# A long convolution's table products as three rounded products in place of one fp32 product

## The chip, the cores and the metric

One core of one Trainium2 chip runs the whole program. The metric is the device time of one execution in microseconds (us). The engines are TensorE (PE; its weight loads are listed apart as PEld), VectorE (DVE), ScalarE (ACT), GpSimd (POOL) and SyncE (SP), which issues most loads.

## The reference

Two layers of a mixed backbone over 640 tokens: 512 latent tokens and 128 context tokens, width 1024. A layer is a feed-forward, a mixer and a second feed-forward. In the mixer one projection feeds three groups of channels: pooling, attention and "Hyena". The last is what matters here; it runs two long convolutions one behind the other, each over the whole sequence:

```python
def fft_conv(z, k):
    L = z.shape[1]
    zf = jnp.fft.rfft(z, n=2 * L, axis=1)
    kf = jnp.fft.rfft(k, n=2 * L, axis=0)
    return jnp.fft.irfft(zf * kf[None], n=2 * L, axis=1)[:, :L]

def hyena_mixer(u, sw, sb, filt, bias_d):
    uc = short_conv(u, sw, sb).astype(F32)
    v, x1, x2 = jnp.split(uc, 3, axis=-1)
    bd = bias_d.astype(F32)
    z = v
    for o, gate in enumerate((x1, x2)):
        z = gate * (fft_conv(z, filt[:, o]) + bd[o] * z)
    return z.astype(u.dtype)
```

## The kernel before

All weight products are three products of rounded parts: a weight tile of 128x512 is loaded (raw), ACT casts it to fp32r (whi, L294), DVE subtracts (wlo, L295), and PE adds hi x hi, lo x hi and hi x lo in fp32r. Each record `mm<-hhi,whi` with 320 columns is one of these. The tokens are the columns, 640 in two halves.

A long convolution has no FFT: the transforms are products with tables of cosines and sines. The generator `conv_step_old` does one convolution of 256 channels (two tiles) for the latent tokens and, with a small table kept in a constant, for the context:

- It asks for four forward tables (tab, 256 KB each, `load_full`, SP's queue) and five tiles of the filter's spectrum (kf), transposes even and odd tokens (ztp) and copies them (zt).
- zf: for two halves of the frequencies (fi = 0, 1) and two parities (pa), four fp32 products of 256 columns. One fp32 product stands in the trace as two records. ACT copies the odd part (zod), DVE adds and subtracts (zp, zm), multiplies by the spectrum (`cmul`: cw, cy) and combines (pp, pmn).
- It asks for four inverse tables, multiplies the context's part (zfc, zcs, cw, cy), and transforms back: yt, 16 fp32 products, and ytc, the context's. ACT scales (yv), DVE adds the bias term and multiplies by the gate (yu, yw).

A layer's two convolutions run one behind the other, as one of several generators (hyena, pooling, attention) whose steps are laid between the weight products by an order written out by hand (the string PROP), fixed when the program is built. Instructions run on each engine in that order. k and q are normalised (nps, qbc, u at L1297) and rotated (L1304 to L1307, "rope") on DVE in the same stretches, and the pooling of two channel groups (pl, pc, pw, pd, L1166 to L1185) stands there too: its small memsets are POOL's, a copy is ACT's, the sums are DVE's.

All these tiles (tables, spectra, zt, pp, pw, ...) come from one pool of 45 buffers (SLOTS, tag "s"). Whoever takes a buffer waits for the last reader of what was in it. The mixer chooses the convolution and, in the attention's step, transposes v (vt) right behind the second one.

Of the kernel before, what the change touches and what calls it, by code (L numbers as in the profile page):

```python
# [11 lines left out]
F32 = mybir.dt.float32  # L12
# [35 lines left out]
PVSKEW = 1  # L48
AHD = 2
PROP = "TGTTTTGGTGSGGGGTGTSTGTGTGSTGTGGSXTSGTSQGQDTGTQGGTTDDSTGTTQGSQGTDDTDTQQSGQQGQQDDQQDDDGTRQGSSDTSGDGGNDQNQSTTTGDGQDTSGQTDTGSGDDQGQDGTQSTQGDNGD"  # L50
CONV3 = 0
SQN = 3
TABX = 1
ADAW = (1.0, 1.25, 2.0, 0.75)
# [128 lines left out]
def hybrid_kernel(ctx: ExitStack, tc: tile.TileContext, a, depth=2, fc=22):  # L183
    nc = tc.nc
    V, S, G, DMA = nc.vector, nc.scalar, nc.gpsimd, nc.sync
# [78 lines left out]
    def load_tables(name, h, n, new=slot):  # L264

        ts = []
        for q in range(n):
            t = new(512, F32R, name="tab")
            DMA.dma_start(out=t.bitcast(F32), in_=a[name][h, q])
            ts.append(t.rearrange("p (h c f) -> p h c f", h=2, c=2))  # L270
        return ts

# [701 lines left out]
    def conv_step(l, o, z, gate, out):  # L974
        rl, rlc = filt[l]
        tf = [load_tables("fwd", 0, 4)]
        kf = filter_tiles(l, o)
        hb = PR(l, "hb")
# [15 lines left out]
        for fi in range(2):  # L994
            eo = []
            for pa in range(2):
                ps = mix(512, "zf")
                for c in range(2):
                    for i in range(2):
                        triple(ps[:, c * 256:(c + 1) * 256], [tf[fi][pa * 2 + i][:, h, c] for h in range(2)],  # L1000
                               [t[:, i, :] for t in zt[pa]], i == 0, i == 1)
                eo.append(ps)
            od = slot(512, name="zod")
            S.copy(out=od, in_=eo[1])
            zp, zm = slot(512, name="zp"), slot(512, name="zm")
            V.tensor_tensor(out=zp, in0=od, in1=eo[0], op=ALU.add)
            V.scalar_tensor_tensor(out=zm, in0=od, scalar=-1.0, in1=eo[0], op0=ALU.mult, op1=ALU.add)
            y = cmul(zp, kf[fi], o, 0)
            yp = cmul(zm, kf[2 + fi], o, 1)
            pp, pm_ = slot3(2, 256, name="pp"), slot3(2, 256, name="pmn")  # L1010
            for q in range(2):
                V.tensor_tensor(out=pp[:, q], in0=y[:, q], in1=yp[:, 1 - q], op=ALU.add)
                V.tensor_tensor(out=pm_[:, q], in0=y[:, q], in1=yp[:, 1 - q], op=ALU.subtract)
            hl = []
            for p_ in (pp, pm_):
                hl.append((slot3(2, 256, F32R, "ph"), slot3(2, 256, F32R, "pl")))
                split(p_, *hl[-1])
            pq.append(hl)
            if fi == 0:
                tf.append(load_tables("fwd", 1, 4))  # L1020
            if fi == 0:
                yield
        ti, vs = [load_tables("back", 0, 4)], []
        psc = mix(512, "zfc")
        for c in range(2):
# [119 lines left out]
    def short_conv(l, ci, u):  # L1145
        sw, sb = PR(l, "sw"), PR(l, "sb")
        t = slot(T, name="sc")
        S.activation(out=t, in_=u, func=AF.Identity, bias=sb[:, ci:ci + 1], scale=sw[:, 6 + ci:7 + ci])
        for c0, c1 in SEG:
            V.scalar_tensor_tensor(out=t[:, c0 + 1:c1], in0=u[:, c0:c1 - 1], scalar=sw[:, ci:ci + 1],  # L1150
                                   in1=t[:, c0 + 1:c1], op0=ALU.mult, op1=ALU.add)
            V.scalar_tensor_tensor(out=t[:, c0:c1 - 1], in0=u[:, c0 + 1:c1], scalar=sw[:, 12 + ci:13 + ci],
                                   in1=t[:, c0:c1 - 1], op0=ALU.mult, op1=ALU.add)
        return t
# [3 lines left out]
    def mixer(l, cur, nxt):  # L1158
# [90 lines left out]
        def need(name):  # L1249
            while name not in made:  # L1250
                next(stream)
            return made[name]
# [227 lines left out]
        def hyena():  # L1480
            zs = [short_conv(l, i, need(f"v{i}")) for i in range(2)]
            for o, (ci, ns) in enumerate(((2, ("xa", "xb")), (4, ("xc", "xd")))):
                out = []
                gate = lambda: [short_conv(l, ci + i, need(n)) for i, n in enumerate(ns)]
                yield from (conv_step if CONV3 else conv_step_old)(l, o, zs, gate, out)
                zs = out
# [320 lines left out]
```

## Time and profile before

| | us |
|---|---|
| median of 3 runs | 2418.3 (2416.39 to 2420.72) |
| the profiled execution | 2417.21 |
| its span, first to last instruction | 2415.4 |
| PE busy in it | 2369.8 (98%) |
| DVE busy | 1920.3 (80%) |
| ACT busy | 1094.6 (45%) |
| POOL busy | 17.8 (1%) |
| granted clock of PE, mean | 0.990 of full speed |

The span is the time between the first and the last instruction that the profiler saw; the execution's own time has 1.8 us around it. Busy shares are averages over stages that have different limits.

### The profile page before, as it was taken

To read this page: it belongs to the slowest core of one execution; us is meant where nothing else is said; L and a number is where in the kernel's file an instruction comes from. 1 tells how busy PE (TensorE), PEld (TensorE's weight loads), DVE (VectorE), ACT (ScalarE), POOL (GpSimd) and SP (SyncE) were. 2 spreads that over 40 slices of the span, in tenths; PEclk is the share of its full clock that TensorE was granted. 3 is DMA by queue.
4 is the path that set the end of the run, shared out by engine and by line. 5 is a ranking of instruction groups with operands and counts; after the bars stand their busy time and mean duration, and the time that the engine had idled before them with its cause. 6 is when DMAs were issued, how large, how long until landed. Compare 5 with 4: busy or idle time off the path is not lost.

```text
span 2415.4 us, 41068 instructions
## 1 busy us (share of the span) xinstructions
PE 2369.8 (98%) x15576; PEld 2246.0 (93%) x15576; DVE 1920.3 (80%) x3885; ACT 1094.6 (45%) x2228; POOL 17.8 (1%) x46
## 2 busy tenths in 40 slices
PE   8999999999989999999999999999998999999999
PEld 3799999999877999999999999999987789999999
DVE  7887888986786798888889889898678678567583
ACT  4653352534345653443535435253434555335251
POOL 0000000000000000000000000000000000000000
PEclk9999999999989999999999999999998999999999
DMA  9434434353210235434343443534231022222222
GB/s 323 168 105 132 134 115 154 101 170 114 102 45 15 78 106 161 127 121 144 117 131 106 124 130 116 164 113 154 89 105 61 18 71 79 79 84 78 85 68 90
DMA packets 132646, 270.37 MB, mean 112 GB/s; under 512 B 15002, under 2 KB 24924, under 8 KB 132320
## 3 DMA queue, kind: packets, MB, share of 16 engines
q1 hardware_dynamic: 132448, 267.75, 34.5%
q8 instruction: 122, 2.00, 0.3%
q14 instruction: 76, 0.62, 0.1%
HBM read 259.56 MB, written 8.13 MB: 111 GB/s over the span
## 4 chain that ended last, share of the span: by engine, by line
PE 93%; DVE 4%; issue 1%; ACT 1%; DMA 1%; SPq 0%; POOL 0%; POOLq 0%; DVEq 0%; ACTq 0%
PE mm L204 79%; PE Z L204 5%; PE yt L204 1%; PE o L204 1%; PE pt L208 1%; PE fk L204 1%; PE mx L204 1%; PE ada L204 1%; PE zf L204 1%; PE rsb L204 0%; PE qbc L204 0%; DMA ar<-in_ada 0%; PE tot L204 0%; DMA par<-in_par 0%; PE nps L204 0%
## 5 line engine op out<-in xcount | busy, mean ns | idle before, releaser
L204 PE MATMUL mm<-hhi,whi 128*128 128x320 f32 x1440 | 448.2, 311 | 1.1 <-ACT u L1220 1.1
L204 PE MATMUL mm<-hlo,whi 128*128 128x320 f32 x1440 | 445.7, 309 | 0.0
L294 ACT CAST whi<-raw 128x512 fp32r<-128x512 f32 (+1 forms) x394 | 238.8, 607 | 456.2 <-PE mm L204 425.9
L204 PE MATMUL mm<-hhi,wlo 128*128 128x320 f32 x1440 | 445.4, 309 | 0.0
L204 PE MATMUL mm<-ahi,whi 128*128 128x320 f32 x1198 | 370.2, 309 | 0.0
L204 PE MATMUL mm<-alo,whi 128*128 128x320 f32 x1198 | 370.2, 309 | 0.0
L204 PE MATMUL mm<-ahi,wlo 128*128 128x320 f32 x1198 | 370.2, 309 | 0.0
L295 DVE TENSOR_TENSOR wlo<-raw,whi 128x512 fp32r<-128x512 f32 (+1 forms) x394 | 262.9, 670 | 77.4 <-ACT whi L294 75.2
L409 DVE CUSTOM_DVE_ANT_0 junk<-araw,condb,par 128x1024 bf16<-128x1024 f32 x240 | 307.1, 1280 | 2.2 <-DMA araw<-in_adat 0.7
L204 PEld LDWEIGHTS mm<-hhi,whi 128*128 128x128 f32 x1440 | 270.3, 188 | 6.0 <-ACT u L1220 2.8
L204 PEld LDWEIGHTS mm<-hlo,whi 128*128 128x128 f32 x1440 | 270.6, 188 | 2.0 <-issue 1.8
L204 PEld LDWEIGHTS mm<-hhi,wlo 128*128 128x128 f32 x1440 | 270.3, 188 | 1.4 <-issue 1.4
L204 PE MATMUL mm<-thi,whi 128*128 128x320 f32 x864 | 267.0, 309 | 0.0
L204 PE MATMUL mm<-tlo,whi 128*128 128x320 f32 x864 | 267.0, 309 | 0.0
L204 PE MATMUL mm<-thi,wlo 128*128 128x320 f32 x864 | 267.0, 309 | 0.0
L204 PEld LDWEIGHTS mm<-ahi,whi 128*128 128x128 f32 x1198 | 224.9, 188 | 0.0
L204 PEld LDWEIGHTS mm<-ahi,wlo 128*128 128x128 f32 x1198 | 224.9, 188 | 0.0
L204 PEld LDWEIGHTS mm<-alo,whi 128*128 128x128 f32 x1198 | 224.9, 188 | 0.0
L294 ACT CAST whi<-ex 128x512 fp32r<-128x512 f32 x216 | 134.2, 621 | 186.9 <-PE mm L204 173.3
L295 DVE TENSOR_TENSOR wlo<-ex,whi 128x512 fp32r<-128x512 f32 x216 | 148.9, 689 | 31.7 <-ACT whi L294 27.2
L294 ACT CAST whi<-ws 128x512 fp32r<-128x512 f32 x144 | 89.4, 621 | 162.2 <-PE mm L204 123.1
L204 PEld LDWEIGHTS mm<-tlo,whi 128*128 128x128 f32 x864 | 162.2, 188 | 0.0
(263 smaller groups left out, 4713.6 us busy)
## 6 DMA issues: line engine op xcount, KB each, us to landing
araw<-in_adat SPq DMA_DIRECT2D x120, 512.0 KB, 3.6
raw<-in_wgu SPq DMA_DIRECT2D x208, 256.0 KB, 3.0
ex<-in_wgu SPq DMA_DIRECT2D x144, 256.0 KB, 2.7
raw<-in_wd SPq DMA_DIRECT2D x128, 256.0 KB, 2.7
raw<-in_win SPq DMA_DIRECT2D x56, 256.0 KB, 2.8
ar<-in_ada SPq DMA_DIRECT2D x48, 256.0 KB, 5.4
raw<-in_wd SPq DMA_DIRECT2D x64, 192.0 KB, 2.6
tab<-in_tfi SPq DMA_DIRECT2D x32, 256.0 KB, 4.1
```

What stands on the lines that cost most here:

```text
L204: cls.order(nc.tensor.matmul(**k))
L208: cls.order(nc.tensor.transpose(**k))
L294: S.copy(out=hi, in_=src)
L295: V.tensor_tensor(out=lo, in0=src, in1=hi.bitcast(F32), op=ALU.subtract)
L409: V.tensor_tensor_reduce(out=junk, in0=raw, in1=condb[:, r], scale=1.0, scalar=bias(l, g)[:, s, c, r:r + 1], op0=ALU.mult, op1=ALU.add, ac ...
```

## The change

A switch selects another generator, and its loader uses another queue:

```diff
--- before.py
+++ after.py
@@ -48,7 +48,7 @@
 PVSKEW = 1
 AHD = 2
 PROP = "TGTTTTGGTGSGGGGTGTSTGTGTGSTGTGGSXTSGTSQGQDTGTQGGTTDDSTGTTQGSQGTDDTDTQQSGQQGQQDDQQDDDGTRQGSSDTSGDGGNDQNQSTTTGDGQDTSGQTDTGSGDDQGQDGTQSTQGDNGD"
-CONV3 = 0
+CONV3 = 1
 SQN = 3
 TABX = 1
 ADAW = (1.0, 1.25, 2.0, 0.75)
@@ -266,7 +266,7 @@
         ts = []
         for q in range(n):
             t = new(512, F32R, name="tab")
-            DMA.dma_start(out=t.bitcast(F32), in_=a[name][h, q])
+            G.dma_start(out=t, in_=a[name][h, q])
             ts.append(t.rearrange("p (h c f) -> p h c f", h=2, c=2))
         return ts
```

`load_tables` was there but unused; with its line changed it is GpSimd that issues the loads, into a tile of type fp32r. The generator `conv_step` differs from `conv_step_old` in these lines ("triple" is the three products of rounded parts):

```python
        tf = [load_tables("fwd", 0, 4)]
...
        zt = [(slot3(2, 256, F32R, name="zt"), slot3(2, 256, F32R, name="ztl")) for _ in range(2)]
...
            split(ps, *(t.rearrange("p a b -> p (a b)") for t in zt[pa]))
...
                        triple(ps[:, c * 256:(c + 1) * 256], [tf[fi][pa * 2 + i][:, h, c] for h in range(2)],
                               [t[:, i, :] for t in zt[pa]], i == 0, i == 1)
...
            for p_ in (pp, pm_):
                hl.append((slot3(2, 256, F32R, "ph"), slot3(2, 256, F32R, "pl")))
                split(p_, *hl[-1])
            pq.append(hl)
            if fi == 0:
                tf.append(load_tables("fwd", 1, 4))
...
        ti, vs = [load_tables("back", 0, 4)], []
...
            if pa == 1:
                ti.append(load_tables("back", 1, 4))
```

A table that holds rounded high and low parts is twice as long: a convolution has 16 loads of 256 KB in place of 8, in four groups of four (forward fi = 0 and 1, inverse pa = 0 and 1). It has 48 + 48 products of 256 columns in fp32r in place of 16 + 16 in fp32 (32 + 32 records), two more splits (zt into zt and ztl) and four more (pp and pmn into ph and pl), each an ACT cast and a DVE subtraction, and 12 more buffers of the 45 in use at one time or another.

What moves is seen at three places, all in layer 0's second convolution. The first is POOL's row of instructions, with what each waits for in brackets (semaphores of the engines and of the DMA queues: DMASW are GpSimd's, DMAHW are SP's). Before, the memsets of the pooling's two channel groups (pl the latent tokens, pc the context):

```order
L1166 MEMSET pl_7436 128x8 [waits DMAHW5_49,DVE_49,Activation_49]
L1167 MEMSET pl_7436 128x8
L1166 MEMSET pc_7437 128x8 [waits DMAHW5_49,DVE_49,PE_49]
L1167 MEMSET pc_7437 128x8
L1166 MEMSET pl_7552 128x8 [waits DMAHW2_49,DVE_49]
L1167 MEMSET pl_7552 128x8
L1166 MEMSET pc_7553 128x8 [waits DMAHW6_49,DVE_49,Activation_49]
L1167 MEMSET pc_7553 128x8
```

The same place after:

```order
L269 DMA tab_7434<-in_fwd 128x512 [waits DMASW4_49,DMAHW3_49,DVE_49,Activation_49]
L269 DMA tab_7436<-in_fwd 128x512 [waits DMASW5_49,DMAHW2_49,DVE_49,PE_49]
L269 DMA tab_7438<-in_fwd 128x512 [waits DMAHW6_49,DMASW6_49,DVE_49]
L269 DMA tab_7440<-in_fwd 128x512 [waits DMASW7_49,DMASW4_49,PE_49]
L1166 MEMSET pl_7572 128x8 [waits DMASW5_49,PE_49]
L1167 MEMSET pl_7572 128x8
L1166 MEMSET pc_7573 128x8 [waits DMASW7_49,PE_49]
L1167 MEMSET pc_7573 128x8
L269 DMA tab_7691<-in_back 128x512 [waits DMASW0_49,DVE_49,Activation_49]
L269 DMA tab_7693<-in_back 128x512 [waits DMASW1_49]
L269 DMA tab_7695<-in_back 128x512 [waits DMASW2_49,DMAHW0_49,DVE_49,PE_49]
L269 DMA tab_7697<-in_back 128x512 [waits DMASW3_49,DVE_49,Pool_49]
```

The table loads now stand in POOL's order, between the pooling's memsets, and each waits for an engine or for an earlier load (tab_7440 for DMASW4, the lane of tab_7434, and for PE).

The second place is PE at zf of fi = 1 (zf_7498 before, zf_7642 after; the number behind a tile's name tells it from others). Before, the end of the run of all zf products:

```order
L204 MATMUL zf_7498<-zt_7167,tab_7152 128x256
L204 MATMUL zf_7498<-zt_7167,tab_7154 128x256
L204 MATMUL mm_7371<-hhi_6075,whi_7375 128x320
L204 MATMUL mm_7371<-hlo_6076,whi_7375 128x320
L204 MATMUL mm_7371<-hhi_6075,wlo_7376 128x320
```

After, where the third table of fi = 1, tab_7438, has been used for the first of two parts of its rows:

```order
L204 MATMUL zf_7642<-ztl_7269,tab_7438 128x256
L204 MATMUL zf_7642<-zt_7268,tab_7438 128x256
L204 MATMUL zfc_7699<-ztc_7284,cst 128x256
L204 MATMUL mm_7597<-hhi_6075,whi_7601 128x320
L204 MATMUL mm_7597<-hlo_6076,whi_7601 128x320
L204 MATMUL mm_7597<-hhi_6075,wlo_7602 128x320
```

and at the end of the 24 weight products that begin there:

```order
L204 MATMUL mm_7598<-hhi_6093,whi_7601 128x320
L204 MATMUL mm_7598<-hlo_6094,whi_7601 128x320
L204 MATMUL mm_7598<-hhi_6093,wlo_7602 128x320
L204 MATMUL zf_7642<-zt_7268,tab_7440 128x256
L204 MATMUL zf_7642<-ztl_7269,tab_7440 128x256
```

Before, both fi's products are one run on the same four tables, with the weight products behind it; after, fi = 1 has tables of its own, and the products with the last one, tab_7440, stand behind 24 weight products.

The third place is PE at the end of the inverse transform. Before, the first channel tile's context product follows its own yt, and the second tile uses the same four tables:

```order
L204 MATMUL yt_7585<-tab_7531,pmn_7301 128x256
L204 MATMUL yt_7585<-tab_7533,pmn_7301 128x256
L204 MATMUL yt_7585<-tab_7535,pmn_7526 128x256
L204 MATMUL yt_7585<-tab_7537,pmn_7526 128x256
L204 MATMUL ytc_7594<-cst,cy_7549 128x128 x2
L204 MATMUL yt_7600<-tab_7531,pp_7300 128x256
L204 MATMUL yt_7600<-tab_7533,pp_7300 128x256
```

After, the rows behind the last product with tab_7697:

```order
L204 MATMUL ytc_7803<-cst,cy_7709 128x128
L204 MATMUL ytc_7809<-cst,cy_7709 128x128
L204 MATMUL yt_7745<-tab_7771,ph_7430 128x256 x2
L204 MATMUL yt_7745<-tab_7771,pl_7431 128x256
L204 MATMUL yt_7745<-tab_7773,ph_7430 128x256 x2
L204 MATMUL yt_7745<-tab_7773,pl_7431 128x256
```

The context products now come ahead of the products with the second four inverse tables (tab_7771 to tab_7777), which belong to pa = 1.

## Rows read from the trace of the kernel before

**Rows 1.** Page, parts 1 and 4: TensorE's time and the chain's shares.

```profile
PE 2369.8 (98%) x15576; PEld 2246.0 (93%) x15576; DVE 1920.3 (80%) x3885; ACT 1094.6 (45%) x2228; POOL 17.8 (1%) x46
...
PE 93%; DVE 4%; issue 1%; ACT 1%; DMA 1%; SPq 0%; POOL 0%; POOLq 0%; DVEq 0%; ACTq 0%
```

**Rows 2.** Groups by form: busy us, mean ns | idle, what ended it.

```profile
L204 PE MATMUL zf<-zt,tab 128*128 128x256 f32 x128 | 28.8, 380 | 2.1 <-ACT zt L1077 2.1
...
L204 PE MATMUL yt<-tab,pp 128*128 128x256 f32 x64 | 19.7, 445 | 7.9 <-DMA tab<-in_tfi 3.5 <-DVE pp L1104 3.2 <-DVE cw L968 1.2
...
L204 PE MATMUL yt<-tab,pmn 128*128 128x256 f32 x64 | 17.5, 423 | 0.0
```

**Rows 3.** Timeline, PE, layer 0's first convolution: start, us, instruction [idle <-releaser].

```profile
581.35 0.31 PE L204 MATMUL mm<-hhi,wlo 128*128 128x320 f32 x1
...
582.23 0.31 PE L204 MATMUL mm<-hhi,wlo 128*128 128x320 f32 x1
582.38 3.61 PE L204 MATMUL zf<-zt,tab 128*128 128x256 f32 x16
585.64 0.49 PE L204 MATMUL mm<-hhi,whi 128*128 128x320 f32 x1
```

**Rows 4.** Timeline, TensorE, layer 0's second convolution and the step behind it.

```profile
654.49 7.17 PE L204 MATMUL zf<-zt,tab 128*128 128x256 f32 x32 [1.05 <-ACT zt L1077]
...
681.21 2.04 PE L204 MATMUL yt<-tab,pp 128*128 128x256 f32 x4 [3.05 <-DMA tab<-in_tfi]
683.72 2.04 PE L204 MATMUL yt<-tab,pp 128*128 128x256 f32 x4 [0.46 <-DMA tab<-in_tfi]
...
692.40 0.71 PE L208 MATMUL vt<-ident,u 128*128 128x128 f32 x5
...
709.86 0.78 PE L208 MATMUL pt<-ident,sc 128*128 128x128 f32 x2 [3.58 <-DVE sc L1353]
```

**Rows 5.** Timeline, TensorE, end of layer 0's first convolution.

```profile
617.26 1.56 PE L204 MATMUL yt<-tab,pp 128*128 128x256 f32 x6
...
624.83 0.81 PE L204 MATMUL qbc<-qn,bind 32*128 32x320 f32 x4
...
637.00 0.39 PE L208 MATMUL ztp<-ident,yw 128*128 128x128 f32 x1 [0.47 <-DVE yw L1141]
```

**Rows 6.** Timeline, VectorE, layer 0's convolutions.

```profile
625.67 1.01 DVE L1297 SCALAR_TENSOR_TENSOR u<-u,par,qbc 128x320 f32<-128x320 f32 x2 [3.21 <-PE qbc L204]
...
663.03 0.69 DVE L1098 TENSOR_TENSOR zp<-zod,zf 128x512 f32<-128x512 f32 x1 [0.45 <-ACT zod L1096]
...
669.46 0.68 DVE L295 TENSOR_TENSOR wlo<-raw,whi 128x512 fp32r<-128x512 f32 x1
670.62 0.71 DVE L1171 TENSOR_TENSOR pw<-pl 128x527 f32<-128x527 f32 x1 [0.48 <-ACT pl L1168]
...
675.09 0.69 DVE L1098 TENSOR_TENSOR zp<-zod,zf 128x512 f32<-128x512 f32 x1
...
682.54 0.69 DVE L966 TENSOR_TENSOR cw<-zcs,kf 128x512 f32<-128x512 f32 x1
...
684.65 0.71 DVE L1171 TENSOR_TENSOR pw<-pl 128x527 f32<-128x527 f32 x1
...
688.61 0.30 DVE L1171 TENSOR_TENSOR pw<-pc 128x143 f32<-128x143 f32 x1
```

**Rows 7.** Timeline, TensorE, layer 1's second convolution.

```profile
1809.61 7.17 PE L204 MATMUL zf<-zt,tab 128*128 128x256 f32 x32 [1.05 <-ACT zt L1077]
...
1848.65 0.71 PE L208 MATMUL vt<-ident,u 128*128 128x128 f32 x5
```

**Rows 8.** Tile tab over the whole span, last line: its loads.

```profile
DMA to landing us min/median/max: 2.8/4.6/6.3
```

**Rows 9.** Page, part 6: loads of the table, KB each, us to landing.

```profile
tab<-in_tfi SPq DMA_DIRECT2D x32, 256.0 KB, 4.1
```

**Rows 10.** Window: busy us (instructions) by engine, granted clock, DMA share, GB/s.

```profile
680.00:690.00 10.00, 8.33 (x27) 6.56 (x28) 9.49 (x24) 2.34 (x6) 0.28 (x4) 0.66 0.42 124
```

## Prediction

> **What bounds the kernel now.** The page's first and fourth parts say which engine sets the end [rows 1]: TensorE (PE) is busy 98% of the span and 93% of the chain that ended last. So a microsecond of PE's streaming can count, and so does any wait that PE does not have today. The grouped lines give the size of what the change works on [rows 2]: the long convolutions' two kinds of table products, zf and yt, are 256 records over four convolutions (two per layer). In the PE timeline 16 of them stand between starts at 582.38 and 585.64 [rows 3], 0.204 us each; a run of 32 takes 7.17 us, 0.22 each [rows 4]. In all 256 x 0.21 = 54 us of PE, 2.2% of the span.
>
> The same timeline shows that a layer's two convolutions are bound differently. In the first, PE goes from weight products into zf and back without a gap [rows 3], and its end is a wait of 0.47 us on VectorE's (DVE's) yw at 637.00 [rows 5]: DVE sets it. In the second PE runs out of other work: it waits 1.05 us ahead of zf, and 3.05 and 0.46 us ahead of yt for an inverse table that lands late [rows 4]. DVE's timeline there is nearly unbroken [rows 6]: combine (zp to pmn), pooling (pw), combine again, the context's product (cw), pooling again. A table whose buffer is freed late in this stretch has nothing left to hide behind; that is what I follow.
>
> **Streaming.** Per convolution 64 records become 48 + 48 rounded products of 256 columns. No row shows one. Rounded weight products of 320 columns start 0.147 us apart (582.23 less 581.35 over six starts [rows 3]). That is the upper bound for 256 columns; in proportion to columns it is 0.117, the lower. I take 0.12, near the proportional end, since these have the same operands and row count and differ in columns alone. 384 x 0.12 = 46 us: a gain of 8 in all, 2.0 per convolution. At 0.147 it is 56 us, no gain. The gain counts only where PE sets the pace.
>
> **First convolution of a layer: 0.** By the changed order its tables have some 7 us or more of other products between asking and use (72 and 91 weight products, then yt with 27), more than the longest landing below, so no table waits. Its 2 us go to DVE's chain: the end waits on yw [rows 5], which does not come earlier. The new order also puts 27 weight products and all 24 yt of the second half ahead of k's qbc. Before, that stretch starts at 617.26 and qbc at 624.83 [rows 5], its u on DVE at 625.67 [rows 6]. After: 617.3 less 1.1 gained in zf, + 24 x 0.12 + 0.44 (ytc) + 27 x 0.147 + 24 x 0.12 = 626.4, and 0.4 for two qbc records: 626.8, so DVE's chain starts 1.1 later. Two zt splits now stand ahead of rope on DVE, about 0.65 each at the pitch of the rows around: 1.3. DVE enters the second convolution 2.4 us late.
>
> **Second convolution, four landings in series.** A layer's tables were eight loads, all asked for early or in one batch of four; now they are sixteen. The second four of each direction are asked for inside the stage, each when a buffer comes free. By the waits of the built program, on layer 0's clock:
>
> - fi=0's combine ends at 669.46 [rows 6] + 2.4 = 671.9. Behind it stand one wlo and two new splits at 0.6 pitch: t0 = 673.7. The second and third tables of fi=1 are asked for behind these splits, and the Pool queue keeps their order.
> - Landing 1, then 6 products of zf_7629 (0.7), the last readers of tab_7434. The fourth table, tab_7440, takes that buffer, so it is asked for at t0 + 0.1 + L (the second table was asked for 0.6 ahead of t0).
> - Landing 2: 24 weight products (3.5 us) are all PE has meanwhile. Then 6 products, 0.7.
> - DVE's pooling now stands behind these reads: 670.62 to 675.09 [rows 6], 4.5, with ACT's copies pl ahead of the zod copy; then combine again, 663.03 to 669.46, 6.4; then wlo and two splits, 1.8.
> - Landing 3: tab_7697 waits for the last of these splits. Then 14 products, 1.7.
> - The context product's remaining 1.5 of its 2.1 us (682.54 to 684.65), pooling to 688.61 + 0.30, 4.3. tab_7777 waits for the buffer that pooling reads.
> - Landing 4, then 14 last products, 1.7.
>
> Without landings: 0.1 + 0.7 + 4.5 + 6.4 + 1.8 + 1.7 + 5.8 + 1.7 = 22.7, so the end is 673.7 + 22.7 + 4L = 696.4 + 4L. Before, the next step (vt) starts at 692.40 [rows 4]: a loss of 4.0 + 4L per layer. Layer 1 has the same rows 1.1 us longer (1809.61 to 1848.65 against 654.49 to 692.40) [rows 7], so I take it twice.
>
> **L.** No row shows a load through GpSimd's queue or one that rounds. Tables of the same 256 KB through SP's queue land after 2.8 to 6.3 us, the filters' tables counted in [rows 8]; the convolutions' have a median of 4.1 [rows 9]. I take 4.1: the size and the pattern are the same, and four at once is how that median arose. Bounds 2.8 and 6.3. What the queue itself adds is the main unknown.
>
> A page of the Trainium skill, "DMA: Bandwidth & Descriptors", section on the anatomy of a DMA on the GpSimd path, gives 2.0 us plus bytes over 436 GB/s; for 256 KB that is 2.6, an estimate by that page, and the sum by it would be about 2446. The rows of SP's queue are longer, and no row here is of that queue.
>
> At 4.1 a layer loses 4.0 + 16.4 = 20.4. PE's clock adds to it: between 680 and 690, where PE idled 3.05 us, the granted clock averages 0.66 [rows 10], the mix of its two levels 1.2 and 2.4 GHz, and four yt there took 2.04 us, where 32 zf at full clock took 7.17 [rows 4], 0.9 for four. Four idle stretches replace one; for the few products between them I add 2.0 (14 products at half clock cost 1.7 more). 22.4 x 2 = 44.8.
>
> **Hidden parts.** The remaining splits (six DVE subtractions and four ACT casts more per convolution) lie in the sum where they stand ahead of a load; on ACT they lie under DVE's chain. Behind the waiting table loads on Pool stand the memsets of pl and pc; ACT's pl copy and then zod queue behind them, and DVE's pw. That is inside the 4.5. 8.4 MB more traffic is 3% of the 270 moved; I cost it at nothing, since weights are loaded ahead in these stretches; without that cover it is 8.4 MB at the 110 GB/s the page averages, shared over the kernel.
>
> **The sum.** The profiled execution took 2417.2 (span 2415.4, 1.8 around it), 1.1 under the median of the runs, 2418.3. 2417.2 + 44.8 = 2462.
>
> **Rivals.**
> *Same.* PE has 45 us without work in the whole span [rows 1], and 3.58 of them stand behind this stage at 709.86, for DVE's sc [rows 4]. If the stage behind runs on its own clock, the delay is given back. Against: one place gives back 3.6 of some 20 per layer, so the stage's delay would have to be under 6, and L under 0.6. Time 2413 to 2422.
> *Faster.* The loads are hidden anyway: DVE reaches the splits and the pooling early enough that buffers are free and tables landed before PE asks for them, so no PE wait is new, and the 8 us of streaming come through: 2417 - 8 = 2409. It decides where a layer's second convolution is no longer than its 38 us of before, so L and the 4.0 of reordering must both vanish. For it: PE's chain share says that streaming counts nearly everywhere. Against: the waits are fixed in the built program, and late tables already cost 3.05 and 0.46 here today.
> *GpSimd's queue is much slower.* If a load through it takes the longest landing seen, 6.3: 4.0 + 25.2 = 29.2 and 3.4 of clock, 32.6 per layer: 2482; with products at 0.147 besides, 2490. For it: DVE is busy in 9.5 of the 10 us of these stretches [rows 10], just when the loads are asked for.
> The Trainium skill, "SBUF — State Buffer", section "Who interferes with whom", says that DVE and GpSimd share a port under an exclusive lock, and that a GpSimd load of 0.62 us took 3.1 beside a DVE copy. By that page an estimate of 2.5 us more per landing gives 4 x 2.5 x 2 = 20 on top, 2482. The operations in rows 6 are two-operand ones, for which no row shows such a lock.
> *The products are no cheaper.* At 0.147 the 2 us of each second convolution vanish and the firsts hold 0.3 more: 2467, inside the range.
>
> **How the numbers follow.** Table waits in the second convolutions (forecast, with products at any pace in the bounds) 0.73; the slow queue 0.13; faster 0.08; same 0.06. Low end: L = 2.8 makes the stage 4.0 + 11.2 + 1.2 (24 weight products then outlast landing 2) = 16.4, less 2.1 if the first convolution keeps its gain, 14.3: 2446; the 3.58 given back in both layers, 2439; 5 more for the two pitches, 2434. High end: 2490 plus the same 5: 2495. Below and above these I leave about 0.15. A measurement of this kernel tells about 0.2% (5 us) from no change. Faster by over that 0.08, within it 0.06, slower 0.86.
>
> **What would show it.** Right: in the changed kernel PE rows of zf<-zt,tab and yt<-tab with idle before them named by tab's DMA, four such per layer near 674, 681, 698 and 711, of 0.5 to 4 us each, and none in the first convolutions; 0.12 between rounded starts; landings through POOL's queue of 3 to 6 us; vt near 713 instead of 692. Wrong: landings under 2 us or over 8, DVE's pooling running ahead of zf's last products, the first convolution with table waits, or a gap at 709.86 that vanishes with the delay.

## The result, and the profile after

The changed kernel is slower: 2476.8 us, median of four runs (2466.8 to 2477.9), against 2419.5 before (four runs); the ratio is 1.0229 with a 95% interval of 1.0200 to 1.0258. The prediction was 2462 with a range of 2434 to 2495. The profiled execution took 2466.8 us, the shortest of the four, 49.6 more than the profiled one of before. What follows reads these two traces; a second trace of the changed kernel (below) has the same waits.

The page of the changed kernel: span, busy times, the new queue, and the forward tables' loads with the median time to landing.

```profile
span 2465.0 us, 41505 instructions
...
PE 2373.1 (96%) x15704; PEld 2253.3 (91%) x15704; DVE 1935.6 (79%) x3909; ACT 1103.8 (45%) x2244; POOL 53.4 (2%) x110
...
q0 software_dynamic: 9216, 16.78, 2.5%
...
tab<-in_fwd POOLq DMA_DIRECT2D x32, 256.0 KB, 3.2
```

PE's busy time is nearly that of before (2369.8 [rows 1]); its share fell from 98% to 96%. So almost all of the 49.6 us is time in which PE does nothing. The waits of PE by cause (us in total, times, longest) say for what:

```profile
PE yt L204 <- DMA tab<-in_back: 30.5, 6, 10.3
PE mm L204 <- ACT u L1220: 13.7, 6, 5.1
...
PE zf L204 <- DMA tab<-in_fwd: 7.0, 4, 2.6
```

Before, PE waited for tables 3.5 us in all [rows 2]. Now it is 30.5 and 7.0, and 13.7 for ACT's copy u. PE's timeline of layer 0's second convolution shows where (start, us, instruction, in brackets the idle time before it and what ended it):

```profile
655.46 0.38 PE L204 MATMUL zf<-zt,tab 128*128 128x256 f32 x1 [1.46 <-ACT zt L294]
664.59 0.63 PE L204 MATMUL mm<-hhi,whi 128*128 128x320 f32 x1 [5.13 <-ACT u L1220]
676.25 0.36 PE L204 MATMUL zf<-zt,tab 128*128 128x256 f32 x1 [2.49 <-DMA tab<-in_fwd]
...
678.15 0.39 PE L204 MATMUL zf<-zt,tab 128*128 128x256 f32 x1 [1.30 <-DMA tab<-in_fwd]
...
701.14 0.77 PE L204 MATMUL yt<-tab,ph 128*128 128x256 f32 x2 [10.01 <-DMA tab<-in_back]
...
707.49 0.71 PE L204 MATMUL ytc<-cst,cy 128*128 128x128 f32 x4 [0.73 <-DVE cy L970]
713.49 0.80 PE L204 MATMUL yt<-tab,ph 128*128 128x256 f32 x2 [4.84 <-DMA tab<-in_back]
...
719.81 0.46 PE L208 MATMUL vt<-ident,u 128*128 128x128 f32 x2
```

The stage that took 37.9 us, from 654.49 to 692.40 [rows 4], now takes 64.3. POOL's queue in the same stretch shows when the tables were asked for, and what each waited for:

```profile
672.43 0.54 POOL L269 DMA_DIRECT2D tab<-in_fwd  x1 [27.93 <-ACT ph L294]
673.64 1.05 POOL L269 DMA_DIRECT2D tab<-in_fwd  x2 [0.67 <-PE mm L204]
679.43 0.53 POOL L269 DMA_DIRECT2D tab<-in_fwd  x1 [4.74 <-PE zf L204]
...
697.50 2.33 POOL L269 DMA_DIRECT2D tab<-in_back  x4 [10.84 <-ACT ph L294]
...
710.45 0.53 POOL L269 DMA_DIRECT2D tab<-in_back  x1 [2.82 <-issue]
...
712.08 1.05 POOL L269 DMA_DIRECT2D tab<-in_back  x2 [0.34 <-DVE pw L1171]
```

DVE's steps between them, to be laid beside [rows 6]:

```profile
665.38 0.69 DVE L1006 TENSOR_TENSOR zp<-zod,zf 128x512 f32<-128x512 f32 x1 [0.45 <-ACT zod L1004]
...
673.02 0.69 DVE L295 TENSOR_TENSOR pl<-pmn,ph 128x512 fp32r<-128x512 f32 x1
...
690.46 0.68 DVE L1006 TENSOR_TENSOR zp<-zod,zf 128x512 f32<-128x512 f32 x1
...
698.08 0.69 DVE L295 TENSOR_TENSOR pl<-pmn,ph 128x512 fp32r<-128x512 f32 x1
705.73 0.69 DVE L966 TENSOR_TENSOR cw<-zcs,kf 128x512 f32<-128x512 f32 x1 [6.96 <-ACT zcs L1028]
```

Read the three together: the two splits of fi = 0 (672.42, not shown, and 673.02) let the second and third table of fi = 1 go (673.64); the second lands at 678.1; six products free the buffer of the fourth (679.43); zf ends, DVE pools and combines (690.46); the splits let the inverse tables go (697.50); their products, the context's cw (705.73) and the pooling let the last four go (710.45 to 713.1); vt follows at 719.81. It is the chain of the prediction. (The POOL row at 673.64 names PE's mm as what came last; in e11 below, where the same loads again go 1.21 us behind the first, its row names the split pl.) Layer 1 does the same, 61.4 us in place of 39.0 [rows 7]:

```profile
1836.72 0.38 PE L204 MATMUL zf<-zt,tab 128*128 128x256 f32 x1 [1.46 <-ACT zt L294]
...
1898.15 0.71 PE L208 MATMUL vt<-ident,u 128*128 128x128 f32 x5
```

The two stages lose 26.4 and 22.4, 48.8 of the 49.6 us.

One thing more. In the first convolution the rounded products start 0.12 us apart (24 of them between these two rows):

```profile
582.15 0.28 PE L204 MATMUL zf<-zt,tab 128*128 128x256 f32 x1
...
584.91 0.28 PE L204 MATMUL zf<-zt,tab 128*128 128x256 f32 x1
```

In the second it is 0.21. The windows of the first convolution's zf and of the two inverse groups (length, busy time and count of PE, PEld, DVE, ACT, POOL, then the granted clock, DMA's share and GB/s) show the clock beside it: 1.00 of full speed in the first, 0.56 and 0.50 behind waits of 10.01 and 4.84 us, near the lower of the two levels, 1.2 GHz in place of 2.4.

```profile
582.00:585.00 3.00, 3.00 (x27) 3.00 (x26) 0.00 (x0) 0.00 (x0) 0.00 (x0) 1.00 0.29 87
701.00:707.00 6.00, 5.58 (x24) 5.11 (x24) 1.27 (x3) 1.19 (x2) 0.14 (x2) 0.56 0.33 95
713.40:719.80 6.40, 6.02 (x24) 5.43 (x25) 1.77 (x7) 0.96 (x2) 0.00 (x0) 0.50 0.41 94
```

### The profile page after: what moved, and what is told of

It reads as the page before. It is cut to its first block, busy times and chain, and to the rows that moved or that the text cites. A ratio compares the mean times of both kernels' runs of the same rounds, so it can differ in the third digit from the quotient of the medians.

```text
span 2465.0 us, 41505 instructions
## 1 busy us (share of the span) xinstructions
PE 2373.1 (96%) x15704; PEld 2253.3 (91%) x15704; DVE 1935.6 (79%) x3909; ACT 1103.8 (45%) x2244; POOL 53.4 (2%) x110
## 5 line engine op out<-in xcount | busy, mean ns | idle before, releaser
L204 PE MATMUL mm<-hhi,whi 128*128 128x320 f32 x1440 | 449.8, 312 | 13.7 <-ACT u L1220 13.7
L295 DVE TENSOR_TENSOR wlo<-ex,whi 128x512 fp32r<-128x512 f32 x216 | 149.0, 690 | 33.8 <-ACT whi L294 29.2
L204 PEld LDWEIGHTS mm<-thi,whi 128*128 128x128 f32 x864 | 162.2, 188 | 0.0
L204 PEld LDWEIGHTS mm<-thi,wlo 128*128 128x128 f32 x864 | 162.2, 188 | 0.0
```

What stands on the lines that cost most here:

```text
L204: cls.order(nc.tensor.matmul(**k))
L295: V.tensor_tensor(out=lo, in0=src, in1=hi.bitcast(F32), op=ALU.subtract)
```

## Experiments

Theory: serial table waits in the second convolutions, with the clock that falls behind each. Rivals: the loads through GpSimd's queue cost something wherever they are; the rounded products and the splits do. The stage's length, from zf's first product to vt's (its last where vt is split up), is the measure that other parts of the kernel blur least; in every run it holds the same 102 products of weights and keys:

| kernel | stage of layer 0, layer 1 (us) | median of runs |
|---|---|---|
| before | 37.9, 39.0 | 2419.5 |
| changed | 64.3, 61.4 | 2476.8 |
| e1, first convolutions alone | 38.5, 40.3 | 2426.5 |
| e2, half the tables | 47.7, 48.8 | 2450.1 |
| e3, asked for early | 51.4, 52.7 | 2461.8 |
| e4, before, GpSimd's queue | 39.0, 39.5 | 2418.9 |
| e5, own table buffers | 43.0, 41.6 | 2466.5 (base 2455.3) |
| e6, base of e5 | 38.8, 39.4 | 2455.3 |
| e7, one product of three | 48.2, 48.6 | 2439.3 |
| e8, feed-forwards' buffers | 53.9, 53.7 | 2456.5 |
| e10, before, late tables early | 41.4, 41.8 | 2428.1 |
| e11, waits filled | 59.9, 61.6 | 2468.7 |
| e12, second convolutions alone | 62.6, 62.9 | 2466.4 |

**e1, the first convolutions alone.**

```diff
-                yield from (conv_step if CONV3 else conv_step_old)(l, o, zs, gate, out)
+                yield from (conv_step if o == 0 else conv_step_old)(l, o, zs, gate, out)
```

> The first convolution of each layer in rounded products, the second as before. Serial table waits in the second convolution (the prediction's theory): the first has no table wait, so 2417 to 2424, 1 us or so per layer over the kernel before. Rival, the loads through GpSimd's queue or the rounded products and splits cost something wherever they are: half of the loss stays, 2440 to 2455.

Measured: 2426.5, ratio 1.0023 (1.0008 to 1.0037), some 6 us over before, a little more than the theory allowed and far from the rivals. No table of the first convolutions makes PE wait. The stage behind them starts 2.9 us later than in [rows 4] and is hardly longer:

```profile
657.42 1.19 PE L204 MATMUL zf<-zt,tab 128*128 128x256 f32 x2 [2.17 <-ACT zt L1077]
...
695.96 0.71 PE L208 MATMUL vt<-ident,u 128*128 128x128 f32 x5
```

**e12, the second convolutions alone** (the same line with `o == 1`).

> The first convolution of each layer as before, the second in rounded products. If the two parts add up, the loss of the whole less the 5 us measured with the first alone: 2466 to 2474. Rival, the first convolutions carry half of it through work that they push into the second: 2445 to 2455.

Measured: 2466.4 (2463.3 to 2476.2), ratio 1.0199 (1.0176 to 1.0223). The two parts add up: the second convolutions carry nearly all of it, in half of the rounded products, splits and loads.

**e4, the queue by itself.** The kernel before, its tables loaded by GpSimd.

```diff
-            DMA.dma_start(out=t.rearrange("p a b -> p (a b)"), in_=a[name][q])
+            (G if name == "tfi" else DMA).dma_start(out=t.rearrange("p a b -> p (a b)"), in_=a[name][q])
```

> The kernel before, its convolution tables (fp32, 32 loads) issued by GpSimd in place of SyncE, nothing else. If the queue itself is no slower than the rows of SyncE's queue, 2416 to 2424. Rival, a slow or contended queue of GpSimd: the late tables of the second convolution come later still, 2430 or more.

Measured: 2418.9, ratio 0.9992 (0.9980 to 1.0004): no difference. The loads land after a median of 3.1 us, sooner than SyncE's 4.1 [rows 9]:

```profile
tab<-in_tfi POOLq DMA_DIRECT2D x32, 256.0 KB, 3.1
```

The rival of a slow queue falls. These loads do not round; the changed kernel's, which do, have 3.2 and 3.5 over the whole kernel.

**e2, half of the tables.**

```diff
-                tf.append(load_tables("fwd", 1, 4))
+                tf.append(tf[0])
...
-                ti.append(load_tables("back", 1, 4))
+                ti.append(ti[0])
```

> The second half of each direction's tables is not loaded; the products of fi = 1 and of pa = 1 use the first half's tables (that part of the computation is changed). All products, splits and the queue stay. Serial waits: landings 1, 2 and 4 go, one landing for the inverse tables stays; 2425 to 2442. Rival, products and splits: 2465 to 2480, no change. Rival, each load through the queue costs: half of it goes, about 2448.

Measured: 2450.1, ratio 1.0129 (1.0109 to 1.0150). All products and splits are there, and half of the loss is gone, so the rival of the products alone falls. The time was higher than the theory's range by 8 us, and it is the number that the third expectation gave for a price on each load, about 2448. This run does not refute that rival; e4 does, where the same queue costs nothing, and so do e8 and e5 below, which keep every load. What the trace shows is that PE still waits 8.60 us for the inverse tables, and that new waits stand behind, 4.22 for yv and 4.87 for the pooling's split plo, which the prediction did not know.

```profile
688.65 0.76 PE L204 MATMUL yt<-tab,ph 128*128 128x256 f32 x2 [8.60 <-DMA tab<-in_back]
701.88 1.33 PE L208 MATMUL vt<-ident,u 128*128 128x128 f32 x5 [4.22 <-ACT yv L1051]
727.81 0.63 PE L204 MATMUL mm<-plo,whi 128*128 128x320 f32 x1 [4.87 <-DVE plo L1196]
```

**e3, the same loads asked for early.**

```diff
-        tf = [load_tables("fwd", 0, 4)]
+        tf = [load_tables("fwd", h, 4) for h in range(2)]
...
-        ti, vs = [load_tables("back", 0, 4)], []
+        ti, vs = [load_tables("back", h, 4) for h in range(2)], []
```

> All eight forward tables are asked for at the start, all eight inverse ones together, from the same 45 buffers. Serial waits: landings 1, 2 and 4 leave the path as far as buffers come free in time, 2428 to 2455. Rivals, products and splits, or a price for each load: no change, 2465 to 2480.

Measured: 2461.8, ratio 1.0181 (1.0155 to 1.0208), between the expectations and above the theory's range. The stages are 13 and 9 us shorter, but PE still waits for the inverse tables (8.4 and 2.0 us in layer 0), and what the stages gain is mostly lost outside them. Of the 45 us that this trace is over the one of before, 27 lie in the two stages; the stretch between them is 11.4 us longer than before (in the changed kernel it is not longer), the end of the kernel 4.8. PE's waits for the pooling's split plo, 8.2 us in all, are a part of that; the rest was not followed up.

**e8, other buffers for the late tables of the second convolutions.**

```diff
-                tf.append(load_tables("fwd", 1, 4))
+                tf.append(load_tables("fwd", 1, 4, extra if o else slot))
...
-                ti.append(load_tables("back", 1, 4))
+                ti.append(load_tables("back", 1, 4, extra if o else slot))
```

> In the second convolutions the tables of fi = 1 and of pa = 1 go into the feed-forwards' buffers, of which two are free then; the first two of each four are asked for some 8 us earlier, the other two wait for these. Serial waits: landing 1 and part of landing 4 go, 2 and 3 stay; 2452 to 2468. Rivals, products and splits, or a price for each load: 2470 to 2480.

Measured: 2456.5 (2448.9 to 2462.7), ratio 1.0154 (1.0124 to 1.0184): 20 us less than the changed kernel with the same products, splits and number of loads. Inside the theory's range.

**e5 and e6, four buffers of the tables' own.** The room comes from other tiles, so e6, the kernel before with the same cuts, is the base.

```diff
-WB = 5
-EXB = 7
...
-RAWB = 4
+WB = 4
+EXB = 6
...
+RAWB = 3
...
-    def load_tables(name, h, n, new=slot):
+    def tabbuf(n, dt, name):
+        return wp.tile([P, n], dt, tag="tab", bufs=4, name=nm(name))
+
+    def load_tables(name, h, n, new=tabbuf):
```

> The changed kernel with four buffers of the tables' own, so that a load waits for the reader of an earlier table alone and not for splits, pooling or combine; to make room the weight tiles have 4 buffers in place of 5, the feed-forwards' extra ones 6 in place of 7, the raw ones 3 in place of 4. To be read against the next run, the kernel before with the same cuts. Serial waits: landings 1 to 3 lie under zf, combine and pooling, the fourth stays with the clock it costs and the first convolutions' 5 us; 10 to 25 us over that run. Rival, products and splits: 45 to 60 us over it. Rival, the queue: the same 45 to 60, with landings over 4 us in the trace.

> The kernel before with the same cuts of the weight tiles' and raw buffers: the base for the run with own table buffers. No theory of the convolutions says anything of it; from 2420 (buffers to spare) to 2480.

Measured: 2466.5 against 2455.3. Ratios to the kernel before are 1.0205 (1.0181 to 1.0229) and 1.0146 (1.0123 to 1.0169), so the change costs 11 us here by the medians, 14 by the ratios, where it cost 57. The stage in e5, then its ends in e6:

```profile
676.51 0.38 PE L204 MATMUL zf<-zt,tab 128*128 128x256 f32 x1 [1.05 <-ACT zt L297]
681.83 0.36 PE L204 MATMUL zf<-zt,tab 128*128 128x256 f32 x1 [1.47 <-DMA tab<-in_fwd]
708.38 1.01 PE L204 MATMUL yt<-tab,ph 128*128 128x256 f32 x3 [3.36 <-ACT ph L297]
719.56 0.79 PE L208 MATMUL vt<-ident,u 128*128 128x128 f32 x5 [3.15 <-ACT yv L1054]
```

```profile
676.68 7.17 PE L204 MATMUL zf<-zt,tab 128*128 128x256 f32 x32 [1.05 <-ACT zt L1077]
...
715.50 0.71 PE L208 MATMUL vt<-ident,u 128*128 128x128 f32 x5
```

It is 4.2 us longer than its base in layer 0 and 2.2 in layer 1, where the changed kernel lost 26.4 and 22.4. Every product, split and load is there. What is gone is a table's wait for the buffer of something else, and that decides it between theory and rivals. It does not single out one wait: PE's waits for ACT's u, 13.7 us in the changed kernel, are gone too, and the built order moves (the first inverse products now stand among weight products at 695). Still there: 1.47 us for a forward table, and 3.36 for a split (ph) ahead of yt. In these two traces the difference is 10.4 us, 6.4 in the stages and 3.6 between them.

**e7, one product of three.**

```diff
-        for n, (lh, rh) in enumerate(((l_[0], r_[0]), (l_[0], r_[1]), (l_[1], r_[0]))):
+        for n, (lh, rh) in enumerate(((l_[0], r_[0]),)):
```

> One of the three rounded products (high by high), the others left out, so the result is less exact; loads, splits and waits stay. Serial waits with a cold clock: 60 products of 0.21 us lie between the landings of a layer's second convolution, 40 of them go, 8.4 us a layer: 2452 to 2464. Rival, landings alone: 2470 to 2480. Rival, the products themselves make the loss: 2440 or less.

Measured: 2439.3, ratio 1.0088 (1.0068 to 1.0109), 37.5 us less than the changed kernel and below what the theory allowed. The number fits the third rival. In layer 0's stage PE is busy 27.9 us, against 38.9 in the changed kernel and 33.8 before, and idle for 20.3, against 25.4 and 4.1. So of the 16.1 us that went, 11.0 are PE's time, 0.17 for each of the 64 products left out, and 5.1 are waits; the theory had counted 40 products. With fewer products the built order changes as well: ahead of yt PE waits 7.21 us for a split with 1.90 for a table behind it, where it was 10.01 for a table. Most of the idle time stays with a third of the products, and in e5 the loss goes with all of them, so the products alone do not make it.

```profile
686.76 1.41 PE L204 MATMUL yt<-tab,ph 128*128 128x256 f32 x4 [7.21 <-DVE pl L295]
690.06 0.77 PE L204 MATMUL yt<-tab,ph 128*128 128x256 f32 x2 [1.90 <-DMA tab<-in_back]
```

**e11, the waits filled with useless products.**

```diff
         for pa in range(2):
+            for _ in range((0, (40, 18)[pa])[o]):
+                PE.matmul(out=yt[0][:, pa * 256:pa * 256 + P], lhsT=ident, rhs=ident, start=True, stop=True)
```

> The changed kernel with products of no use (128 x 128, fp32, into a buffer that is written anew) in the second convolutions, 40 ahead of the first inverse products and 18 ahead of the second, about as long as PE waits there, 8.8 and 4.0 us; the table waits are the same. If the half clock behind a wait is a part of the loss, the 48 inverse products come 0.12 in place of 0.21 us apart, 4 us a layer: 2464 to 2472, though PE does more. If only the landings count: 2474 to 2482.

Measured: 2468.7 (2463.1 to 2476.6), ratio 1.0206 (1.0182 to 1.0231). That is in the range of the clock's theory, but the runs overlap those of the changed kernel, so the time alone settles nothing. The trace says more: the filling runs (two records each), the tables' waits ahead of the two groups of layer 0 shrink to 0.49 and 1.34 us, and the inverse products behind them start 0.12 apart at a granted clock of 1.00, not 0.21 at 0.50 to 0.56.

```profile
689.99 9.09 PE L204 MATMUL yt<-ident 128*128 128x128 f32 x80
...
703.64 0.50 PE L204 MATMUL yt<-tab,ph 128*128 128x256 f32 x2 [0.49 <-DMA tab<-in_back]
...
714.62 0.50 PE L204 MATMUL yt<-tab,ph 128*128 128x256 f32 x2 [1.34 <-DMA tab<-in_back]
```

```profile
703.60:708.00 4.40, 3.72 (x27) 3.36 (x28) 2.27 (x6) 1.21 (x2) 0.14 (x2) 1.00 0.67 193
714.60:719.00 4.40, 3.36 (x26) 3.13 (x26) 1.53 (x6) 0.07 (x1) 0.00 (x0) 1.00 0.53 156
```

Layer 1's first group ran at 1.00 too. Its last products did not: from 1895.82 they start 0.21 apart again, at 0.52, though the wait ahead of that group was filled as well:

```profile
1898.03 0.63 PE L204 MATMUL yt<-tab,ph 128*128 128x256 f32 x2
1898.45 0.41 PE L204 MATMUL yt<-tab,pl 128*128 128x256 f32 x1
1898.67 0.63 PE L204 MATMUL yt<-tab,ph 128*128 128x256 f32 x2
```

From the first yt to vt the stage is 2.6 us shorter than in the changed kernel in layer 0 and 1.6 in layer 1, with 58 useless products more. Ahead of the first yt the built order moved too (24 weight products now stand behind the filling): the first yt comes 1.9 us sooner behind zf's start in layer 0, and 1.8 later in layer 1 (45.4 us, 43.7 in the changed kernel). So of the 4.4 us that layer 0's stage is shorter, 2.6 can be the clock's.

**e10, the idea turned on the kernel before:** its late inverse tables asked for early.

```diff
+            if fi == 0:
+                ti.extend(load_full(4, 8))
             od = slot(512, name="zod")
...
-        ti, vs = load_full(4, 8), []
+        vs = []
```

> The kernel before with its four inverse tables asked for behind the zf products of fi = 0, ahead of the combine, some 15 us earlier; nothing else. If the late tables alone hold PE in layer 0's second convolution (3.05 and 0.46 us), 2414 to 2417. If DVE's pp is next at the same time, as layer 1's wait of 3.20 us on pp says, no change: 2417 to 2422.

Measured: 2428.1, ratio 1.0032 (1.0019 to 1.0045). Both expectations were wrong. The tables no longer keep PE waiting, but all tiles behind take other buffers of the 45, and the order of the program moves with it. zm now takes a forward table's buffer and waits 2.75 us for its last reader, the four last zf records, which stand behind weight products (PE, then DVE):

```profile
658.45 6.31 PE L204 MATMUL zf<-zt,tab 128*128 128x256 f32 x28 [1.05 <-ACT zt L1077]
...
673.33 1.02 PE L204 MATMUL zf<-zt,tab 128*128 128x256 f32 x4
```

```profile
673.96 0.69 DVE L1102 SCALAR_TENSOR_TENSOR zm<-zod,zf 128x512 f32<-128x512 f32 x1 [2.75 <-PE zf L204]
```

**e9, the changed kernel once more.**

> The changed kernel once more, for a second trace of it: the profiled execution was some 10 us shorter than the median of its runs. Serial waits: the second convolutions have the same waits in the same places, and the difference lies in how long the loads take to land or in the granted clock there; 2466 to 2478.

Measured: 2469.5, span 2467.7. The same waits in the same places (yt 9.93 and 4.88 us in layer 0, vt at 719.77), and the 2.7 us more come between layer 0's vt and layer 1's second zf, outside the second convolutions. No trace was had of an execution at 2476 to 2478, as three of the four timed ones were; what they do otherwise stays open.

No version here beats the kernel before.

## Why the prediction came out as it did

The direction, the range and the mechanism were right: four landings in series in each second convolution, each behind a buffer that was freed late. The time forecast was 5 us under the traced execution and 15 under the median. Layer 1's stage lost 22.4 us, just what was forecast for each, layer 0's 26.4; the granted clock over the stage was 0.81 in layer 1 and 0.76 in layer 0. Step by step, on layer 0's clock:

| step | predicted, us | measured, us |
|---|---|---|
| last split of fi = 0 (t0) | 673.7 | 673.6 |
| landing 1 and six products | 4.2 | 5.8 (to 679.4) |
| landing 2 and six products | 4.8 | 6.9 (to 686.3) |
| pooling, up to zp | 4.5 | 4.2 |
| combine and splits | 8.2 | 8.2 (to 698.7) |
| landing 3 and products | 5.8 | 8.1 |
| cw and pooling | 5.8 | 5.8 |
| landing 4 and products | 5.8 | 7.2 |
| vt | 712.8, with the clock 714.8 | 719.8 |

- *Late entry of DVE, 2.4 us:* right. zp came at 665.38, not 663.03 [rows 6].
- *DVE's steps:* right to 0.3 us. Rows of before that are only moved keep their durations.
- *Landing, 4.1 us:* right in this stage, in part by luck: the row taken was SyncE's, and by GpSimd's queue the same tables land after 3.1 in e4, after 3.2 and 3.5 over the whole changed kernel. But the twelve loads of layer 0's stage took longer (`DMA to landing us min/median/max: 2.9/4.0/5.2`): landings 1, 3 and 4 took 4.5, 4.1 and 4.0. Landing 2 took 2.9 and was hidden.
- *Requests:* 1.1 us not in the sum. The second table was asked for 0.5 us behind the end of its split, and the fourth inverse table stood 0.6 behind its split, since GpSimd issues the four one after the other (697.50 to 699.3).
- *Clock, 2.0 us a layer:* this is the term that was mis-sized. All four steps with a landing took longer than the sum, 7.4 us together, and some 6 of these are products. The six behind landing 1 took 1.3 us, not 0.7. Behind landing 2 came the rest of zf's first part and two context products (1.3), the 24 weight products (4.5, not 3.5) and nine products, not six (1.1). The last products behind landings 3 and 4 took 3.4 and 3.2 us, not 1.7, since they ran 0.21 us apart, not 0.12. The 48 inverse products alone cost 48 x 0.09 = 4.3 us by that spacing, an estimate; e11, which filled the waits, had 2.6 of it back in layer 0 and 1.6 in layer 1.
- *First convolutions, 0:* nearly right in the changed kernel, whose trace has 0.8 us outside the two stages. The streaming gain is real (0.12), and DVE's chain swallows it, as said. Alone, in e1, they cost 6 us, 2.9 of them ahead of layer 0's stage.
- *PE's wait for u, 5.13 us:* not forecast. PE's weight products start later for it, but t0 is DVE's and came as forecast, so it is not on the chain.
- *Products at 0.12 and no table wait in the first convolutions:* right.
- *Rivals:* the slow queue is refuted by e4. Faster and same are refuted by the result. The Trainium skill's estimate of 2.6 us for such a load ("DMA: Bandwidth & Descriptors", anatomy on the GpSimd path) lies under the measured medians of 3.1 to 3.5. The Trainium skill's lock between DVE and GpSimd ("SBUF — State Buffer", "Who interferes with whom"; the load that took 3.1 us in place of 0.62 stands in that page's section "A bandwidth-pool intuition that's wrong (but worth ruling out)") added no 2.5 us to each landing here: the medians are 3.2 and 3.5, the shortest landing 2.7. Whether the longest landing, 5.4, owes something to it is not shown.
- *Two figures of the working:* the 2446 for the shorter landing leaves out the 2.0 us of clock, with which it is 2450; and 2482 with products at 0.147 is 2487 by the working's own 5 us, not 2490. Neither moves the forecast, and the second would lower the upper end by 3.

What is shown and what is argued: that the waits for buffers make the loss is shown by e5, with e2 and e8 beside it; that the products cost 0.21 at the lower clock and 0.12 at the full one is shown by the windows of the changed kernel and of e11. That the wait ahead brings the lower clock is shown for three of e11's four groups; why the fourth fell is open. How the 57 us of the median divide to the last few microseconds is not shown: e5 leaves 11 to 14, of which the splits, the last waits and the first convolutions were not told apart.

## What to carry to other kernels

Here a load cost what its wait for a buffer cost. When a change doubles the number of loads that share a rotating pool with the work between them, look up for each load which instruction frees its buffer, and put these waits in a row; the share of busy time and the transfer time say nothing of it. Count behind each such wait all products that can't start before it, at the lower clock's spacing. And moving one allocation in a rotating pool moves everyone's buffer behind it (e10), so an earlier request can make another wait.

## What the runs showed of the hardware

- GpSimd's queue delivered the same 256 KB tables sooner than SyncE's: 3.1 us median against 4.1. GpSimd was busy 0.53 to 0.56 us with each issue, 2.33 for four of the changed kernel's. Its loads from one stage of the changed kernel landed after 2.9 to 5.2 us, so the median of a whole kernel was not the price on the chain (4.0 to 4.5).
- Products of 256 columns in rounded fp32 start 0.12 us apart at a granted clock of 1.00 and 0.21 at 0.50 to 0.56. With the idle time ahead of them filled by useless products, three of four groups ran at 1.00; the last one fell to 0.52 all the same.
